# The first sublayer's modulation, norm and projections run by pairs of contraction blocks

## The chip, the cores and the metric

The kernel runs as one program on one core of a Trainium2 chip. The metric is device time in microseconds (us) of one execution; the median of a few runs is compared. TensorE (PE) multiplies matrices, VectorE (DVE) and ScalarE (ACT) work elementwise, GpSimd (POOL) does small elementwise work, and SyncE (SP) issues most of the transfers. Each engine works off its own queue in order and waits on semaphores for the others.

## What is computed

A two-layer transformer block for 256 tokens of width 1024 in float32, followed by a second block (convolutions, neighbourhood attention, a mixture of experts). Only the beginning of the first layer matters here:

```
cond = silu(c)
mod  = cond @ ada_w[0] + ada_b[0]
sh1, sc1, g1, sh2, sc2, g2 = split(mod, 6)
h = x * rsqrt(mean(x*x) + eps) * norm_mix[0] * (1 + sc1) + sh1
u = h @ w_in                       # 1024 x 2976, "even_w_in"
c_q, c_kv, k_r, u_dil = u[:384], u[384:640], u[640:672], u[672:]
q, kv = rms_norm(c_q) @ w_uq, rms_norm(c_kv) @ w_ukv
```

After that come the attention over q, k, v and the dilated attention over u_dil.

## The kernel before

**Weights.** All matrices stream through five buffers of 1 MB (`raw`). `fetch` (L219) issues one transfer on SP for two parts of 512 KB each; `pump(n)` (L253) takes the next parts of one fixed list, `seq`. For a weight part ACT makes a rounded copy (`whi`, L268) and DVE the remainder (`wlo`, L270), and each product is three matmuls (`mm3`, L343: whi with th, wlo with th, whi with tl, where th and tl are the same two halves of the activations). For a part of the modulation matrix (`Ada`) DVE multiplies it with the row silu(c) (`rc`) and sums (`ada_part`, L302): a product of 128x1024 for each block of 128 output columns. When all eight blocks of a vector are there, one small step adds the bias (L312). A buffer is free again when its last DVE step is done.

**Staging.** The list begins with the 16 modulation parts of shift and scale, then come the weights of the projection in six column groups ("ein", 0) to ("ein", 5) of 512 columns (the last has 416), with the smaller matrices `uq` and `ukv` behind the third. Meanwhile PE transposes x, ACT takes the sums of squares (`raw_part`, L459) and DVE the root (`rstd2`, L473); `normT` (L508) then scales the eight transposed blocks with the modulation columns and splits them into th and tl. `proj` (L563) runs one column group over all eight contraction blocks, into two accumulators `pg`, one for each half of the tokens, which `evac` empties on ACT. After group 0 `late_consts` (L866) makes sine and cosine, from which POOL makes the rope tables (`rope_tables`, L657). After group 1 the latents are normed, and after group 2 they are turned and split (`lh`, `ll`) and multiplied with `uq` and `ukv`; groups 3 and 4 follow, and group 5 runs among the attention.

**Setup.** `start` (L782) issues the small transfers on three queues and turns rows of parameters into columns (`turn`: a transpose on PE and a copy on DVE); `rest` turns those that are needed later. Within the rules set by these calls a scheduler fixes each engine's order when the program is built.

Of the kernel before, what the change touches and what calls it, by code (L numbers as in the profile page):

```python
# [37 lines left out]

PACK = {"mlp_w1": (512, "c"), "mlp_w2": (D, "k"), "even_w_in": (512, "k"), "even_w_out": (D, "k"),
        "mla_w_uq": (768, "k"), "mla_w_ukv": (1024, "k"), "odd_w_in": (512, "k"), "odd_w_out": (D, "k"),  # L40
# [4 lines left out]
def packed(w, width, mode):  # L45


    out = []
    for m in w:
        K, N = m.shape  # L50
        m = m.reshape(K // 128, 128, N)
        for c0 in range(0, N, width):
            c = m[:, :, c0:c0 + width]
            if mode == "k":
                per = 2 * max(1, SUB // c.shape[2])
                out += [c[k:k + per].transpose(1, 0, 2).ravel() for k in range(0, len(c), per)]
            else:
                out += [c[:, :, j:j + 256].transpose(1, 0, 2).ravel() for j in range(0, c.shape[2], 256)]
    return np.concatenate(out)
# [50 lines left out]
def dram(ap, off, dims):  # L110
    return bass.AP(tensor=ap.tensor, offset=ap.offset + off, ap=dims)
# [44 lines left out]
class Ada:  # L156
# [3 lines left out]
    def __init__(self, key, src, vec, outs, also=None):  # L160
        self.key, self.src, self.runs = key, src, [(vec, outs)] + ([also] if also else [])
        self.row = key[2] in (2, 5)
        self.n = KB
        self.held = False
        self.raw = {}


class Net:
# [30 lines left out]

    def setup_stream(self, groups):  # L200

        self.seq, self.keys, self.held = [], {}, set()
        for main, side, *late in groups:
            for it in main + side:
                self.keys[it.key] = it
            m, s = ([(it, j) for it in l for j in range(it.n)] for l in (main, side))
            if late:
                late[1] = [it.key for it, _ in m].index(late[1])
                h = len(self.seq) + late[1] + len(s) - late[0]
                self.held |= set(range(h, h + late[0]))  # L210
            self.seq += spread(m, s, *late)
        self.pos = 0
        self.done = 0
# [86 lines left out]
    def ada_part(self, it, j, src):  # L300
        nc = self.nc
        if not it.row:  # L302
            if j == 0:
                it.acc = [self.sm.tile([128, 8], F32, name="msum", tag="msum") for _ in it.runs]
            for r, (vec, (dst, bias, plus)) in enumerate(it.runs):
                acc = it.acc[r]
                out = src if r == len(it.runs) - 1 else self.new_acc()
                self.order(nc.vector.scalar_tensor_tensor(out, src, 1.0, self.crow[vec], op0=ALU.mult, op1=ALU.mult,
                                                          accum_out=acc[:, j:j + 1]))
                if j == it.n - 1:  # L310
                    bias = self.col[bias[0]][:, bias[1]:bias[1] + 8]
                    self.order(nc.vector.scalar_tensor_tensor(dst, acc, plus, bias, op0=ALU.add, op1=ALU.add))  # L312
            return
# [455 lines left out]
    def start(self):  # L769
# [46 lines left out]
        def turn(srcs, t):  # L816
            n = t.shape[0]
            p = self.ps.tile([128, 512], F32, name="pt", tag="t")
            self.tp(p[:, :n], t)
            c = cn.tile([128, n], F32, name=srcs[0][0] + "c")  # L820
            nc.vector.tensor_copy(c, p[:, :n])
            r = 0
            for nm, _, k in srcs:
                self.col[nm] = c[:, r:r + k]
                r += k
            return c

        self.b1s = ExitStack()
        self.b1 = self.b1s.enter_context(self.tc.tile_pool(name="b1", bufs=1, side="right", reuse_waits="tile"))
        self.R0 = self.big.tile([128, D], F32, name="R0", tag="gate", bufs=self.gate_bufs)[:, 0:T]  # L830
        self.crow_tiles(None, ["c"], nc.scalar)
        first = [("c", I["c"], 8)]
        bias = [("ada_b", I["ada_b"], 96)]
        more = [("nmix", I["norm_mix"], 16), ("nmlp", I["norm_mlp"], 16), ("ng", I["norm_g_2"], 32),
                ("c2", I["c_2"], 8), ("cctx", I["c_ctx_2"], 8),
                ("qlat", I["mla_q_lat_norm"], 3), ("kvlat", I["mla_kv_lat_norm"], 2), ("subln", I["diff_subln"], 1)]
        bias2 = [("b_ada_2", I["b_ada_2"], 96)]
        r1 = rows(first, nc.sync)
        nc.scalar.dma_start(self.eye, C["eye"])
        r2 = rows(bias, nc.scalar)  # L840
        for t in range(2):
            nc.gpsimd.dma_start(self.x[:, t], dram(I["x"], t * 128 * D, [[D, 128], [1, D]]))
        r3 = rows(more, nc.gpsimd)
        r4 = rows(bias2, nc.gpsimd)
        cs = cn.tile([128, 24], F32, name="cs")
        self.vec = {"c": cs[:, 0:8], "c2": cs[:, 8:16], "cctx": cs[:, 16:24]}
        nc.scalar.activation(self.vec["c"], turn(first, r1), AF.Silu)
        turn(bias, r2)

        def rest():  # L850
            turn(more, r3)
            turn(bias2, r4)
            nc.scalar.activation(self.vec["c2"], self.col["c2"], AF.Silu)
            nc.scalar.activation(self.vec["cctx"], self.col["cctx"], AF.Silu)

        self.rest = rest
        self.ones = cn.tile([128, 128], F32, name="ones")
# [110 lines left out]
class Block1:  # L968
# [9 lines left out]
    def even_items(self):  # L978
        n = self.n
        a = [self.w_items("even_w_in", ("ein", i), 0, D, 2976, i * 512, min(512, 2976 - i * 512)) for i in range(6)]  # L980
# [4 lines left out]
        return a[:3] + [uq, ukv] + a[3:] + o  # L985

    def even(self):
        n, nc = self.n, self.n.nc
        hT = n.normT(n.x, n.modA(0, 0, n.col["nmix"][:, 0:8]), R=n.R0)
        with ExitStack() as es:  # L990
# [28 lines left out]
            ulat = lat.tile([128, 2, D], F32, name="ulat")  # L1019
            n.proj(("ein", 0), hT, KB, 512, evac(0))  # L1020
            n.late_consts()
            n.proj(("ein", 1), hT, KB, 512, evac(1))
            tmp = n.big.tile([128, 2, D], F32, name="tmp", tag="xn")
# [6 lines left out]
            for t in range(2):  # L1030
                nc.vector.tensor_scalar(tmp[:, t, :384], ulat[:, t, :384], ss[:, 0, t:t + 1], None, op0=ALU.mult)
                nc.vector.tensor_scalar(tmp[:, t, 384:640], ulat[:, t, 384:640], ss[:, 1, t:t + 1], None, op0=ALU.mult)
            n.proj(("ein", 2), hT, KB, 512, evac(2))
            tq, tk, tdq, tdk = (n.rope_tables(g, d, rd, t)
# [76 lines left out]

            dil(3)
            dil(4)
# [1098 lines left out]
def build(ctx, tc, I, C, out, probe=None, upto=99):  # L2212
# [21 lines left out]
    first = net.ada_items(0, 0, [0, 1], "c")  # L2234
    net.setup_stream([([], first)] + [(ws(), *side) for _, ws, *side in steps])
    net.pump(6)
    net.raw_start()
    for t in range(2):
        for hf in range(2):
            net.raw_part(net.x, t, hf)  # L2240
    R = net.spread_rows(net.rstd2(net.raw[1]))
    net.nc.scalar.copy(net.R0, R)
    net.pump(16)
    net.flush()
    net.pump(18)
    net.rest()
    net.hooks = {}
# [73 lines left out]
```

## Time and profile before

| | us |
|---|---|
| runs (three) | 2309.50, 2309.63, 2305.48 |
| median | 2309.5 |
| profiled execution | 2298.07 |
| its span | 2296.2 |
| PE busy in it | 2186.0 (95%) |
| DVE busy in it | 1918.0 (84%) |
| ACT busy in it | 1382.8 (60%) |
| POOL busy in it | 198.9 (9%) |

The span is the profiler's from the first to the last instruction. Busy times are sums over the whole span; a matmul counts as busy while it is in the pipe, so PE may be busy and not at its peak. Waits are told by the engine that ended them.

### The profile page before, as it was taken

How to read it: one execution, taken by the hardware profiler on the slowest of the kernel's cores; microseconds unless marked ns; L12 is line 12 of the kernel's file. 1: busy time of each engine (PE TensorE's matmuls, PEld its weight loads, DVE VectorE, ACT ScalarE, POOL GpSimd, SP SyncE). 2: the span in 40 equal slices, each digit the busy share in tenths (PEclk: the TensorE clock that was granted, in tenths of full speed). 3: DMA queues.
4: the chain of work that ended last, by engine and by line, in shares of the span. 5: the costliest groups of instructions: out<-in, count | busy, mean ns of one | idle time of the engine just before them, and what ended most of it. 6: DMA issues, size and time to landing. Idle time of an engine off the chain costs nothing. (4 is left out here: it accounts for less than half of the span.)

```text
span 2296.2 us, 30679 instructions
## 1 busy us (share of the span) xinstructions
PE 2186.0 (95%) x11405; PEld 1802.1 (78%) x11405; DVE 1918.0 (84%) x2602; ACT 1382.8 (60%) x1890; POOL 198.9 (9%) x280
## 2 busy tenths in 40 slices
PE   4998999999999999999999999999999999999997
PEld 3866888676889886589987888888888788788875
DVE  7887988787997668579856899999898889898996
ACT  4644545546645536254444787787777777777764
POOL 2310010311100121200000000000000000000010
PEclk9988999999999999999999999999999999999998
DMA  8554998643677596279925899999989899898981
GB/s 336 186 173 159 336 356 327 188 165 130 245 283 290 187 335 153 74 290 379 384 99 226 342 353 370 341 368 353 349 327 367 326 367 350 338 360 338 370 309 49
DMA packets 102397, 647.44 MB, mean 282 GB/s; under 512 B 12101, under 2 KB 19749, under 8 KB 28128
## 3 DMA queue, kind: packets, MB, share of 16 engines
q1 hardware_dynamic: 88512, 618.83, 71.3%
q0 software_dynamic: 13040, 25.41, 4.5%
q8 instruction: 91, 1.49, 0.2%
q10 hardware_dynamic: 688, 1.16, 0.2%
q14 instruction: 66, 0.54, 0.1%
HBM read 637.21 MB, written 8.15 MB: 281 GB/s over the span
## 5 line engine op out<-in xcount | busy, mean ns | idle before, releaser
L270 DVE TENSOR_TENSOR wlo<-raw,whi 128x1024 fp32r<-128x1024 f32 (+1 forms) x551 | 662.4, 1228 | 123.2 <-ACT whi L268 115.1
L268 ACT CAST whi<-raw 128x1024 fp32r<-128x1024 f32 (+1 forms) x551 | 562.0, 1049 | 335.7 <-PE pg L347 96.8
L270 DVE TENSOR_TENSOR wlo<-rawm,whi 128x1024 fp32r<-128x1024 f32 x422 | 506.0, 1238 | 37.1 <-ACT whi L268 25.4
L268 ACT CAST whi<-rawm 128x1024 fp32r<-128x1024 f32 x422 | 426.2, 1051 | 82.7 <-PE sc L348 29.9
L346 PE MATMUL pg<-th,whi 128*128 128x256 f32 x1024 | 293.0, 290 | 2.2 <-ACT th L527 1.5
L347 PE MATMUL pg<-tl,whi 128*128 128x256 f32 x1024 | 292.7, 286 | 0.5 <-DVE tl L522 0.5
L348 PE MATMUL pg<-th,wlo 128*128 128x256 f32 x1024 | 292.4, 286 | 0.4 <-DVE wlo L270 0.4
L346 PEld LDWEIGHTS pg<-th,whi 128*128 128x128 f32 x1024 | 197.7, 195 | 8.8 <-issue 3.6
L347 PEld LDWEIGHTS pg<-tl,whi 128*128 128x128 f32 x1024 | 199.5, 195 | 4.4 <-issue 2.0
L348 PEld LDWEIGHTS pg<-th,wlo 128*128 128x128 f32 x1024 | 199.4, 195 | 1.4 <-DVE wlo L270 1.2
L347 PE MATMUL sc<-wlo,xo 128*128 128x512 f32 x448 | 179.1, 400 | 8.4 <-DVE wlo L270 8.4
L347 PE MATMUL sc<-wlo,th 128*128 128x512 f32 x448 | 176.9, 395 | 2.8 <-DVE wlo L270 2.8
L348 PE MATMUL pg<-whi,gg 128*128 128x512 f32 x448 | 176.0, 394 | 3.5 <-PEq L2141 3.5
L347 PE MATMUL pg<-wlo,gg 128*128 128x512 f32 x448 | 178.8, 399 | 0.0
L346 PE MATMUL sc<-whi,xo 128*128 128x512 f32 x448 | 176.9, 395 | 0.0
L346 PE MATMUL sc<-whi,th 128*128 128x512 f32 x448 | 176.3, 394 | 0.0
L348 PE MATMUL sc<-whi,xo 128*128 128x512 f32 x448 | 175.7, 392 | 0.0
L348 PE MATMUL sc<-whi,th 128*128 128x512 f32 x448 | 174.9, 390 | 0.7 <-POOL th L2037 0.7
L346 PE MATMUL pg<-whi,gg 128*128 128x512 f32 x448 | 161.1, 392 | 1.4 <-ACT gg L369 1.4
L347 PE MATMUL po<-wlo,ah 128*128 128x512 f32 x344 | 134.3, 391 | 1.4 <-DVE wlo L270 1.4
L346 PE MATMUL po<-whi,ah 128*128 128x512 f32 x344 | 135.2, 393 | 0.0
L348 PE MATMUL po<-whi,al 128*128 128x512 f32 x344 | 133.9, 389 | 0.0
(587 smaller groups left out, 3888.8 us busy)
## 6 DMA issues: line engine op xcount, KB each, us to landing
rawm<-in_moe_w SPq DMA_DIRECT2D x196, 1024.0 KB, 6.6
raw<-in_moe_w SPq DMA_DIRECT2D x140, 1024.0 KB, 6.3
raw<-in_mlp_w SPq DMA_DIRECT2D x64, 1024.0 KB, 6.7
raw<-in_ada_w SPq DMA_DIRECT2D x48, 1024.0 KB, 7.2
raw<-in_w_ada SPq DMA_DIRECT2D x35, 1024.0 KB, 6.9
raw<-in_ffn_w SPq DMA_DIRECT2D x20, 1024.0 KB, 8.2
rawm<-in_w_ada SPq DMA_DIRECT2D x13, 1024.0 KB, 6.9
rawm<-in_ffn_w SPq DMA_DIRECT2D x13, 1024.0 KB, 8.4
```

The lines of the kernel that those rows point to most:

```text
L268: self.order(self.nc.scalar.copy(h, src))
L270: self.order((self.nc.gpsimd if pool else self.nc.vector).tensor_sub(l, src, h.bitcast(F32)))
L346: mm(out, a[0], b[0], start=start, stop=False, skip_group_check=True)
L347: mm(out, a[0], b[1], start=False, stop=False, skip_group_check=True)
L348: return mm(out, a[1], b[0], start=False, stop=stop, skip_group_check=True)
```

## The change

The first norm and the column groups 0 to 2 run in one loop over four pairs of contraction blocks. For each pair the list now holds two parts of shift, two of scale, two weight parts of 1024 columns (groups 0 and 1 in one) and one of 512 columns (group 2). `Ada` gets `per`, so that the bias step works on two columns at a time. The products of a pair go into six accumulators: two `py` tiles of two banks, and two `pg`. The norm is taken before the loop as a diagonal matrix (`dg`), which PE multiplies with x; ACT scales and shifts (`hf`), rounds (`th`), and DVE takes the remainder (`tl`). Group 3 is projected directly behind the loop's latents, ahead of `uq`. x is fetched on SP ahead of the weights, the condition row c for the columns on POOL, and the broadcast row `rc` behind three small transfers on ACT's queue. `rest` is called after the first pair's matmuls.

```diff
-PACK = {"mlp_w1": (512, "c"), "mlp_w2": (D, "k"), "even_w_in": (512, "k"), "even_w_out": (D, "k"),
+PACK = {"mlp_w1": (512, "c"), "mlp_w2": (D, "k"), "even_w_in": ((D, 512, 512, 512, 416), "k"), "even_w_out": (D, "k"),
...
-                if j == it.n - 1:
-                    bias = self.col[bias[0]][:, bias[1]:bias[1] + 8]
-                    self.order(nc.vector.scalar_tensor_tensor(dst, acc, plus, bias, op0=ALU.add, op1=ALU.add))
+                if (j + 1) % it.per == 0:
+                    a, b = j + 1 - it.per, j + 1
+                    bias = self.col[bias[0]][:, bias[1] + a:bias[1] + b]
+                    self.order(nc.vector.scalar_tensor_tensor(dst[:, a:b], acc[:, a:b], plus, bias, op0=ALU.add, op1=ALU.add))
...
-        self.R0 = self.big.tile([128, D], F32, name="R0", tag="gate", bufs=self.gate_bufs)[:, 0:T]
-        self.crow_tiles(None, ["c"], nc.scalar)
...
-        r1 = rows(first, nc.sync)
         nc.scalar.dma_start(self.eye, C["eye"])
         r2 = rows(bias, nc.scalar)
+        self.crow_tiles(None, ["c"], nc.scalar)
         for t in range(2):
-            nc.gpsimd.dma_start(self.x[:, t], dram(I["x"], t * 128 * D, [[D, 128], [1, D]]))
+            self.order(nc.sync.dma_start(self.x[:, t], dram(I["x"], t * 128 * D, [[D, 128], [1, D]])))
+        r1 = rows(first, nc.gpsimd)
...
-        nc.scalar.activation(self.vec["c"], turn(first, r1), AF.Silu)
-        turn(bias, r2)

         def rest():
+            nc.scalar.activation(self.vec["c"], turn(first, r1), AF.Silu)
             turn(more, r3)
             turn(bias2, r4)
...
+    def first(self, ps, done):
+        n, nc = self.n, self.n.nc
+        hi, lo = (n.big.tile([128, KB, T], F32R, name=nm, tag=nm) for nm in ("th", "tl"))
+        A = n.sm.tile([128, 8], F32, name="mA", tag="mA")
+        B = n.mod[:, 0, 0]
+        dg = n.diag(n.x)
+        (ia, ib) = self.head
+        def turned(p):
+            z = n.ps.tile([128, 2, T], F32, name="pt", tag="t")
+            for k in range(2):
+                for t in range(2):
+                    c = (2 * p + k) * 128
+                    n.mm(z[:, k, t * 128:(t + 1) * 128], n.x[:, t, c:c + 128], dg[:, t])
+            return z
+        z = turned(0)
+        for p in range(KB // 2):
+            s = slice(2 * p, 2 * p + 2)
+            if p == 0:
+                n.pump(1)
+                n.bias()
+            n.pump(7 * p + 4)
+            n.order(nc.vector.tensor_tensor(A[:, s], n.mod[:, 0, 1, s], n.col["nmix"][:, s], ALU.mult))
+            n.pump(7 * p + 5)
+            f = n.big.tile([128, 2, T], F32, name="hf", tag="hf", bufs=2)
+            for i, k in enumerate((2 * p, 2 * p + 1)):
+                n.order(nc.scalar.activation(f[:, i], z[:, i], AF.Identity, scale=A[:, k:k + 1], bias=B[:, k:k + 1]))
+                n.order(nc.scalar.copy(hi[:, k], f[:, i]))
+                n.order(nc.vector.tensor_tensor(lo[:, k], f[:, i], hi[:, k].bitcast(F32), ALU.subtract))
+            n.pump(7 * p + 7)
+            if p < KB // 2 - 1:
+                z = turned(p + 1)
+            for k in (2 * p, 2 * p + 1):
...
+                for g in (2, 0, 1):
+                    for t in range(2):
+                        n.mm3(ps[g][t], (hi[:, k, t * 128:(t + 1) * 128], lo[:, k, t * 128:(t + 1) * 128]), w[g], k == 0, k == KB - 1)
+            if p == 0:
+                n.rest()
...
-            n.proj(("ein", 0), hT, KB, 512, evac(0))
+            hT = self.first([[x[:, 0], x[:, 1]] for x in wide] + [[n.ps.tile([128, 512], F32, name="pg", tag="g") for _ in range(2)]],
+                            [evac(i) for i in range(3)])
             n.late_consts()
-            n.proj(("ein", 1), hT, KB, 512, evac(1))
...
-            n.proj(("ein", 2), hT, KB, 512, evac(2))
+            n.proj(("ein", 3), hT, KB, 512, evac(3))
...
-            dil(3)
             dil(4)
```

DVE's queue at the program's start (`raw,msum<-raw,rc` is a modulation product, `rms` the row norm's small steps). Before, the products lead:

```order
L821 COPY cc<-pt 128x8
L821 COPY ada_bc<-pt 128x96
L308 SCALAR_TENSOR_TENSOR raw,msum<-raw,rc 128x1024 x6
L481 TENSOR_SCALAR rms<-ssq 128x1 x2
L483 TENSOR_SCALAR rms<-rms 128x1 x2
```

In the changed program, from the last of the norm's steps on:

```order
L442 SCALAR_TENSOR_TENSOR rms<-rms 128x1 x2
L453 TENSOR_SCALAR dg<-eye,rms 128x128 x2
L312 SCALAR_TENSOR_TENSOR raw,msum<-raw,rc 128x1024
L826 COPY ada_bc<-pt 128x112
L312 SCALAR_TENSOR_TENSOR raw,msum<-raw,rc 128x1024
```

The whole norm moved ahead of the first product.

DVE's queue behind the first pair in the changed program (`cc`, `nmlpc` and `b_ada_2c` are what `rest` copies; PE's transposes for them stand behind the first pair's 36 matmuls):

```order
L274 TENSOR_TENSOR wlo<-raw,whi 128x1024
L1022 TENSOR_TENSOR tl<-hf,th 128x256 x2
L274 TENSOR_TENSOR wlo<-raw,whi 128x1024 x2
L826 COPY cc<-pt 128x8
L826 COPY nmlpc<-pt 128x70
L826 COPY b_ada_2c<-pt 128x96
L312 SCALAR_TENSOR_TENSOR raw,msum<-raw,rc 128x1024 x2
L317 SCALAR_TENSOR_TENSOR mod<-msum,ada_bc 128x2
```

Before, the same copies lay between products, and PE's transposes for them ahead of every weight matmul. Now they lie between PE's first burst and the second pair's products.

ACT's queue around sine and cosine, before (`ulat` and `ud` are what `evac` fills):

```order
L361 COPY ulat<-pg 128x512
L268 CAST whi<-raw 128x1024
L1026 ACTIVATE tmp,lss<-ulat 128x384
L268 CAST whi<-raw 128x1024
L404 ACTIVATE sin<-ang 128x64
L409 ACTIVATE cos<-angt 128x64
```

And in the changed program:

```order
L272 CAST whi<-raw 128x1024 x5
L1056 COPY ud<-pg 128x512 x2
L366 COPY ulat<-py 128x512 x2
L1078 ACTIVATE tmp,lss<-ulat 128x384
L366 COPY ulat<-py 128x160
L1056 COPY ud<-py 128x352
L1079 ACTIVATE tmp,lss<-ulat 128x256
L1078 ACTIVATE tmp,lss<-ulat 128x384
L1056 COPY ud<-py 128x352
L409 ACTIVATE sin<-ang 128x64
L414 ACTIVATE cos<-angt 128x64
```

The cosine moved from behind group 0 to behind the emptying of all three groups.

## Rows read from the trace of the kernel before

**Rows 1.** Stages: us, busy time of each engine, granted clock, DMA share, GB/s.

```profile
13.20:38.00 24.80, 5.52 (x23) 3.79 (x21) 24.49 (x63) 6.72 (x15) 6.21 (x11) 1.00 1.01 396
38.00:62.00 24.00, 23.82 (x96) 18.88 (x97) 22.11 (x50) 16.24 (x27) 5.04 (x15) 1.00 0.68 260
62.00:73.30 11.30, 11.30 (x51) 9.12 (x50) 5.85 (x20) 4.41 (x11) 7.92 (x33) 1.00 0.27 94
73.30:113.00 39.70, 38.98 (x199) 32.49 (x198) 36.67 (x58) 29.46 (x40) 5.84 (x5) 1.00 0.61 216
113.00:140.00 27.00, 25.00 (x173) 21.82 (x171) 26.89 (x50) 14.26 (x39) 7.33 (x9) 1.00 0.44 152
140.00:200.00 60.00, 54.19 (x228) 33.74 (x229) 43.17 (x84) 22.63 (x50) 0.00 (x0) 0.77 0.52 180
```

**Rows 2.** DVE in order of time: start, duration, line, out<-in, idle before.

```profile
13.22 1.22 DVE L308 SCALAR_TENSOR_TENSOR raw<-raw,rc 128x1024 f32<-128x1024 f32 x1
...
20.10 0.33 DVE L481 TENSOR_SCALAR rms<-ssq 128x1 f32<-128x1 f32 x2
...
22.28 1.22 DVE L308 SCALAR_TENSOR_TENSOR raw<-raw,rc 128x1024 f32<-128x1024 f32 x1
```

**Rows 3.** Transfers: issuing queue, count, size, us from issue to landing.

```profile
rc<-in_c ACTq DMA_DIRECT2D x1, 512.0 KB, 4.5
...
eye<-const_eye ACTq DMA_DIRECT2D x1, 64.0 KB, 8.3
stage<-in_ada_b ACTq DMA_DIRECT2D x1, 48.0 KB, 10.9
```

**Rows 4.** ACT at the start: the Silu of the row, the first square.

```profile
5.29 1.06 ACT L896 ACTIVATE rc<-rc 128x1024 f32<-128x1024 f32 x1 [1.88 <-DMA rc<-in_c]
...
11.30 0.63 ACT L467 ACTIVATE raw<-x 128x512 f32<-128x512 f32 x1 [0.99 <-DMA x<-in_x]
```

**Rows 5.** PE's first weight matmuls in order of time.

```profile
38.99 0.63 PE L348 MATMUL pg<-whi,tl 128*128 128x512 f32 x1
...
39.42 0.63 PE L346 MATMUL pg<-whi,th 128*128 128x512 f32 x1
...
43.44 0.39 PE L348 MATMUL pg<-whi,tl 128*128 128x512 f32 x1
...
43.66 0.39 PE L346 MATMUL pg<-whi,th 128*128 128x512 f32 x1
```

**Rows 6.** A transpose of the setup on PE and its copy on DVE.

```profile
9.62 0.24 PE L355 MATMUL pt<-eye,stage 8*128 8x8 f32 x1 [9.62 <-DMA eye<-const_eye]
9.90 0.17 DVE L821 COPY cc<-pt 128x8 f32<-128x8 f32 x1 [0.16 <-PE pt L355]
```

**Rows 7.** Weight rows, casts and the splitting of activations on DVE and ACT.

```profile
43.24 4.83 ACT L268 CAST whi<-raw 128x1024 fp32r<-128x1024 f32 x5
...
44.31 5.77 DVE L270 TENSOR_TENSOR wlo<-raw,whi 128x1024 fp32r<-128x1024 f32 x5 [0.45 <-ACT whi L268]
...
74.92 0.43 DVE L560 TENSOR_TENSOR ll<-hf,lh 128x256 fp32r<-128x256 f32 x1
...
75.46 0.48 ACT L556 ACTIVATE hf<-pt,nmixc 128x256 f32<-128x256 f32 x1 [0.54 <-DVE ll L560]
```

**Rows 8.** The cosine on ACT, and DVE's two kr steps that wait for POOL's tables.

```profile
56.63 0.26 ACT L409 ACTIVATE cos<-angt 128x64 f32<-128x64 f32 x1 [1.25 <-DVE angt L408]
...
63.21 0.23 DVE L1052 TENSOR_TENSOR kr<-ulat,tkA 128x64 f32<-128x64 f32 x1 [0.55 <-POOL tkA L669]
...
69.21 0.23 DVE L1053 TENSOR_TENSOR kr<-kr,kt 128x64 f32<-128x64 f32 x1 [4.23 <-POOL kt L681]
```

**Rows 9.** DVE's marks behind the latents: first lh, qss, second hss.

```profile
74.59 0.29 DVE L559 CAST lh<-hf 128x256 fp32r<-128x256 f32 x1 [0.98 <-ACT hf L556]
...
85.54 1.74 DVE L1088 TENSOR_REDUCE qss<-tmp 128x16 f32<-128x1536 f32 x1
...
112.80 1.75 DVE L693 TENSOR_REDUCE hss<-tmp 128x24 f32<-128x1536 f32 x1
```

More of the change, by code (lines that the diff above doesn't have):

```diff
@@ L48, in packed @@
     out = []
+    widths = width if isinstance(width, tuple) else (w.shape[2] // width) * (width,)
+    assert sum(widths) == w.shape[2]
     for m in w:
@@ L51, in packed @@
         m = m.reshape(K // 128, 128, N)
-        for c0 in range(0, N, width):
+        for i, width in enumerate(widths):
+            c0 = sum(widths[:i])
             c = m[:, :, c0:c0 + width]
@@ L162, in __init__ @@
         self.row = key[2] in (2, 5)
-        self.n = KB
+        self.n = self.per = KB
         self.held = False
@@ L196, in probe, with setup_stream @@
             self.nc.gpsimd.dma_start(self.probe_out[name], ap)
-    def setup_stream(self, groups):
-        self.seq, self.keys, self.held = [], {}, set()
+    def setup_stream(self, head, groups):
+        self.seq, self.keys, self.held = list(head), {it.key: it for it, _ in head}, set()
         for main, side, *late in groups:
@@ L820, in turn @@
             c = cn.tile([128, n], F32, name=srcs[0][0] + "c")
-            nc.vector.tensor_copy(c, p[:, :n])
+            self.order(nc.vector.tensor_copy(c, p[:, :n]))
             r = 0
@@ L829, in start @@
         self.b1 = self.b1s.enter_context(self.tc.tile_pool(name="b1", bufs=1, side="right", reuse_waits="tile"))
-        self.R0 = self.big.tile([128, D], F32, name="R0", tag="gate", bufs=self.gate_bufs)[:, 0:T]
-        self.crow_tiles(None, ["c"], nc.scalar)
         first = [("c", I["c"], 8)]
-        bias = [("ada_b", I["ada_b"], 96)]
-        more = [("nmix", I["norm_mix"], 16), ("nmlp", I["norm_mlp"], 16), ("ng", I["norm_g_2"], 32),
+        bias = [("ada_b", I["ada_b"], 96), ("nmix", I["norm_mix"], 16)]
+        more = [("nmlp", I["norm_mlp"], 16), ("ng", I["norm_g_2"], 32),
                 ("c2", I["c_2"], 8), ("cctx", I["c_ctx_2"], 8),
@@ L854, in rest @@
             nc.scalar.activation(self.vec["cctx"], self.col["cctx"], AF.Silu)
-        self.rest = rest
+        self.rest, self.bias = rest, lambda: turn(bias, r2)
         self.ones = cn.tile([128, 128], F32, name="ones")
@@ L979, in even_items @@
         n = self.n
-        a = [self.w_items("even_w_in", ("ein", i), 0, D, 2976, i * 512, min(512, 2976 - i * 512)) for i in range(6)]
+        a = [self.w_items("even_w_in", ("ein", i), 0, D, 2976, i * 512, w) for i, w in ((0, D), (2, 512), (3, 512), (4, 512), (5, 416))]
+        self.head = a[:2]
         uq = Chunk(("uq",), (n.I["mla_w_uq"], 0), 3, 768, "k")
@@ L984, in even_items @@
              for i, k in ((0, 4), (1, 2))]
-        return a[:3] + [uq, ukv] + a[3:] + o
+        return a[2:3] + [uq, ukv] + a[3:] + o
+    def first(self, ps, done):
[30 more added lines that the diff above has]
+            for k in (2 * p, 2 * p + 1):
+                (ah, al), (bh, bl) = ia.parts[k], ib.parts[p]
+                w = [(ah[:, 0, :512], al[:, 0, :512]), (ah[:, 0, 512:], al[:, 0, 512:]), (bh[:, k % 2], bl[:, k % 2])]
+                for g in (2, 0, 1):
[3 more added lines that the diff above has]
+                n.rest()
+        for g in (2, 0, 1):
+            for t in range(2):
+                done[g](t, ps[g][t])
+        return hi, lo
     def even(self):
         n, nc = self.n, self.n.nc
-        hT = n.normT(n.x, n.modA(0, 0, n.col["nmix"][:, 0:8]), R=n.R0)
         with ExitStack() as es:
@@ L1019, in even @@
             ulat = lat.tile([128, 2, D], F32, name="ulat")
-            n.proj(("ein", 0), hT, KB, 512, evac(0))
+            wide = [n.pa.tile([128, 2, 512], F32, name="py", tag="acc") for _ in range(2)]
+            hT = self.first([[x[:, 0], x[:, 1]] for x in wide] + [[n.ps.tile([128, 512], F32, name="pg", tag="g") for _ in range(2)]],
+                            [evac(i) for i in range(3)])
             n.late_consts()
-            n.proj(("ein", 1), hT, KB, 512, evac(1))
             tmp = n.big.tile([128, 2, D], F32, name="tmp", tag="xn")
@@ L2234, in build @@
     first = net.ada_items(0, 0, [0, 1], "c")
[L2235 to L2246, printed above, removed]
+    for it in first:
+        it.per = 2
+    groups = [(ws(), *side) for _, ws, *side in steps]
+    wide, narrow = b1.head
+    head = []
+    for p in range(KB // 2):
+        head += [(it, 2 * p + j) for it in (*first, wide) for j in range(2)] + [(narrow, p)]
+    net.setup_stream(head, groups)
     net.hooks = {}
```

## The prediction

> **What bounds the kernel now.** I read the stages first [rows 1], then the queues inside the first 113 us. The program differs from the one before only up to about 200 us; from PE's last attention transposes on, every engine's instructions stand in the same order. So the change is worth what it moves in that head, and the remaining 2096 us are carried along unchanged. In the head VectorE (DVE) is the engine that is late. From 13.2 to 38 us it is busy 24.49 of 24.80, with the modulation columns and the row norm; DMA is full as well (share 1.01), but every landed megabyte waits for DVE. TensorE (PE) is busy 5.52 of these 24.80 and starts its first projection at 38. From 113 to 140 DVE is busy 26.89 of 27.00. In between, from 38 to 113, DVE has 10.4 us free (1.9, 5.5 and 3.0 in the three rows). A change that lets PE start early therefore gains only what it takes off DVE's work, or out of DVE's waits, up to 113.
>
> **The start.** DVE's first modulation product starts at 13.22 now [rows 2]. The change puts the row norm ahead of it, in DVE's order and in ScalarE's (ACT): the Silu of the condition row, four squares, 16 small DVE steps and two diagonals. The condition row now leaves ACT's DMA queue as fourth, behind the unit matrix, the biases and the norm weights, where it was first. As first it landed 4.5 us after its issue, and the third of that queue after 10.9 [rows 3]. Issued at about 2.1 it lands between 6.6 and 13.0. I take 10.2, because the unit matrix and the biases needed 3 to 4 us each behind it, while the activations lead SP's queue and are there sooner. The Silu takes 1.06, the four squares 0.63 each [rows 4], the 16 steps 0.1 each (22 took 2.2, from 20.10 to 22.28 [rows 2]), the diagonals about 0.3: 10.2 + 1.1 + 2.5 + 1.6 + 0.3 gives **15.7**, and 12.1 to 18.5 by the bounds.
>
> The Trainium skill, "DMA: Bandwidth & Descriptors", section on queues, rings and completion order, says that an engine takes descriptors of one ring in order and changes between rings at packets. By that rule the row cannot overtake the three that now stand ahead of it, and the nearer end is the late one; the rows agree, since the unit matrix landed behind the row although it is an eighth of its size [rows 3].
>
> **The four pairs.** One pair costs DVE four products of 1.15 (six took 6.9 us [rows 2]), four small steps of 0.4 together, three weight rows of 1.15 (five took 5.77) and two of the low parts of 0.35 (the 0.43 of the row, overlapped) [rows 7]: 9.15. Behind the columns ACT must make hf, th, hf, th (four of 0.43) and then the cast of the next weights (0.97) before the second weight row may start, 2.75 after the columns, when DVE has filled only 2.0 of it. So a pair takes 9.9; pair 0, which also copies the biases, takes 10.2 and ends at 25.9.
>
> Then comes a wait which the profile of before doesn't have. The closing setup (three transposes and three copies of small rows) moved from between the products to behind pair 0's 36 matmuls on PE, and DVE's three copies stand ahead of pair 1's products. PE starts pair 0 at 21.9, when its columns and th are there. The first matmuls of a burst stood 0.43 apart (512 columns at 1.2 GHz) and later ones 0.23 (2.4 GHz) [rows 5]. Pair 0 waits at 26.0 for its narrow weight row with 25 matmuls left: 26.0 + 25 x 0.23 = 31.7. Three rounds of transpose and copy at 0.6 each (0.45 in the rows, and the way back [rows 6]) give 33.5. **DVE stands still for 7.6 us.** Queued behind it are pair 1's products, and behind these SP's fetches, which wait for the buffers. Bounds: 36 matmuls at 0.23 end at 30.2, at 0.43 at 37.4; I take the mixed value, since the row shows this change of pace in the same kind of burst. From 33.5 three pairs of 9.9 end at **63.2**. DMA has landed what they need by then: at the 396 GB/s of the first stage [rows 1] a megabyte takes 2.7 us, so a buffer released at 35.8 is filled again well ahead of its use at 45.8.
>
> The Trainium skill, "TensorE: Matmul & The Clock Gate", section on HAM oscillation, says that matmuls in bursts with waits between them begin each burst at half rate. It speaks against this change. The row agrees for a burst's beginning: 0.43 at 39, 0.23 at 43, [rows 5], in a stage whose granted clock reads 1.00 [rows 1]. By it pairs 2 and 3 would each lose another 1.6 us of PE time, which ends in the next wait below and adds nothing to the sum; what it makes of pair 0 is a rival.
>
> **From the pairs to the latents.** PE has 17 matmuls behind the last weight row: 63.2 + 17 x 0.23 = 67.1. All three projections end together, so ACT empties six accumulators in a row, and only behind them comes the cosine: seven steps of about 0.45 put its end at 70.2, where it is 56.89 now [rows 8]. POOL builds its tables from it: 6.3 us to the one that the first kr step needs (56.89 to 63.2), 12.3 to kr's second step (69.21) [rows 8]. In the changed order DVE's first kr step stands ahead of the latents' scaling and of four weight rows. It is reached at 71.5 and waits until 76.5, **5.0 us**. From there 7.6 us of DVE work follow (four weight rows, 3.8; the latents' scaling and small steps, 3.8), to 84.1, past kr's second wait at 82.5. The fourth quarter of the next projection (512 columns, now ahead of the latents) needs a weight row at 79.7; its 12 matmuls end at 82.4 (0.23) to 84.8 (0.43), and I take 84.0, since PE has waited 4 us. The first lh cast comes 1.6 later, at **85.7**; it is at 74.59 now [rows 9].
>
> **What comes back.** That projection is already done: 48 matmuls (10.9 us) on PE and four weight rows (4.6) on DVE which before lay behind lh. From lh to the qss reduction it is 10.95 now (74.59 to 85.54 [rows 9]), set by the up projection on PE, and unchanged: 96.6. From there to 112.80 DVE runs 27.3 without a gap; four rows less make 22.7: **119.3 against 112.8, +6.5**. PE stands at +0.5: 85.7 + 0.5 to the up projection, and then as before less one projection, the last fourth starting at 99.3 for 98.6 now. The row scaling that falls away on DVE (eight steps of 0.4) is simply absent from the 9.15. From 113 to 140 DVE is full, so the +6.5 stays; behind 200 us nothing differs.
>
> The profiled execution took 2298.1 us, the median of the three runs is 2309.5. The sum in the profiled execution is 2298.1 + 6.5 = 2304.6; carried to the median it is **2316.0**. By its own bounds (start -3.6 to +2.8, pair 0 -1.5 to +5.7, the fourth quarter -1.6 to +0.8, the ACT wait of a pair 0 instead of 0.75, -2.3 in three) it lies at 2311 to 2321.
>
> **Rivals.** (1) PE, not DVE, ends the attention stage. From 140 to 200 PE is busy 54.19 of 60 and DVE 43.17, and DVE's 17 free microseconds could take up its lateness; then only PE's +0.5 is left: **2310**, no change. Against it: PE waits there for softmax rows which DVE makes. It decides if DVE's free time in 140 to 200 shrinks by 6. (2) Faster: TensorE's level. Its granted clock in 140 to 200 is 0.77 [rows 1]; at full speed 54.19 x 0.23 = 12.5 us of it would go. If the other arrangement of transposes and scores keeps it up, 6.5 - 12.5 gives **2303.5**. For it: the transposes and scores of two units now stand closer. Against it: the same matmuls with the same partners. It decides from a granted clock over 0.9 in this stage. (3) Pair 0 never comes to the fast pace, because it waits for weight rows while it starts: 36 x 0.43 ends it at 37.4, +5.7, **2321.7**.
>
> **Chances.** Forecast 0.47, rival 1 0.28, rival 2 0.10, rival 3 0.15. A measurement of this kernel can tell about 0.2%, 4.6 us, from no change. Of the forecast 0.07 lies within that, of rival 1 0.02 below and 0.26 within: faster 0.12, same 0.33, slower 0.55. The range takes in rivals 1 and 3 and reaches to rival 2: 2303 to 2324.
>
> **What would show it.** First weight matmul near 22 us; DVE idle 7 to 8 us ahead of the copy into cc; the first projection's end at 67 and the cosine at 70; DVE idle about 5 us for POOL ahead of kr; first lh near 86, the first score reduction near 121. If DVE doesn't wait at the copy, or starts its products near 12, the step is wrong and the result is no change or a gain; if all these come and the last attention stage still starts no later than now, it is rival 1.

## The result

The changed kernel takes 2326.8 us in the median of six runs (2320.6 to 2335.2), the kernel before 2305.8 in six (2302.1 to 2309.6): 1.0101 times as long, 95% interval 1.0077 to 1.0126. It is slower, as forecast, but by 21 us and not by 6.5, and outside the range, which ended at 2324. The profiled execution took 2330.3 us (span 2328.4), 32 us more than that of before. That one was a quick run of its kernel: 80 runs of before, taken beside the experiments below, have a median of 2306.1.

The stages of [rows 1] in the changed kernel (us, busy time of PE, PEld, DVE, ACT, POOL, granted clock, DMA share, GB/s), and as the last line a stage that is used throughout: from DVE's k norm (`k<-k,qss`) to the first weight matmul of the next sublayer, the attention with its output projection.

```profile
13.20:38.00 24.80, 16.14 (x62) 12.52 (x63) 13.80 (x43) 8.45 (x17) 1.70 (x3) 1.00 0.70 254
38.00:62.00 24.00, 18.88 (x77) 15.07 (x76) 21.75 (x40) 9.59 (x14) 0.00 (x0) 0.79 0.86 326
73.30:113.00 39.70, 34.47 (x155) 28.81 (x155) 30.96 (x66) 25.18 (x45) 20.31 (x52) 0.96 0.51 188
140.00:200.00 60.00, 54.83 (x235) 36.13 (x233) 37.77 (x79) 17.28 (x44) 0.00 (x0) 0.61 0.52 184
119.88:247.72 127.84, 110.28 (x490) 76.59 (x491) 88.75 (x184) 49.18 (x111) 10.35 (x12) 0.75 0.42 149
```

The same stage in the kernel before:

```profile
106.15:222.47 116.32, 105.00 (x529) 74.96 (x528) 89.43 (x185) 53.74 (x116) 10.36 (x12) 0.87 0.49 173
```

PE starts 13 us earlier, but DVE, busy 24.49 of the first 24.80 us in [rows 1], is busy only 13.80 now. The k norm comes at 119.88 where it came at 106.15: **13.7 us of lateness from the head**. The stage behind it holds 39 matmuls fewer and takes 127.8 us where it took 116.3: **11.5 us more**, at a granted clock of 0.75 for 0.87. With two levels, 1.2 and 2.4 GHz, that is 2 x 0.25 x 127.8 = 64 us at the lower one, for 30. The clock of the whole execution, which every run gives, points the same way: 0.965 to 0.970 in the six runs of the changed kernel, 0.971 to 0.980 in the 80 of before. Behind this stage the two profiles differ by 7 us more, which I don't count to the change: from there to the end it took 2074 us in before, 2081 here, and 2070 to 2084 in its variants below, so one profile differs from another there by as much.

DVE's marks in the changed kernel, in order of time (start, duration, line, out<-in, idle before and what ended it). They answer [rows 2], [rows 8] and [rows 9]:

```profile
17.58 1.22 DVE L312 SCALAR_TENSOR_TENSOR raw<-raw,rc 128x1024 f32<-128x1024 f32 x1
...
35.83 0.17 DVE L826 COPY cc<-pt 128x8 f32<-128x8 f32 x1 [6.38 <-PE pt L360]
...
37.17 1.22 DVE L312 SCALAR_TENSOR_TENSOR raw<-raw,rc 128x1024 f32<-128x1024 f32 x1
...
45.42 2.36 DVE L274 TENSOR_TENSOR wlo<-raw,whi 128x1024 fp32r<-128x1024 f32 x2 [0.52 <-ACT whi L272]
...
47.69 1.22 DVE L312 SCALAR_TENSOR_TENSOR raw<-raw,rc 128x1024 f32<-128x1024 f32 x1
...
79.75 0.27 DVE L1104 TENSOR_TENSOR kr<-ulat,tkA 128x64 f32<-128x64 f32 x1 [2.94 <-POOL tkA L674]
...
88.65 0.23 DVE L1105 TENSOR_TENSOR kr<-kr,kt 128x64 f32<-128x64 f32 x1 [2.20 <-POOL kt L686]
...
90.00 0.28 DVE L564 CAST lh<-hf 128x256 fp32r<-128x256 f32 x1
...
102.41 1.74 DVE L1140 TENSOR_REDUCE qss<-tmp 128x16 f32<-128x1536 f32 x1
...
119.88 1.76 DVE L1145 TENSOR_TENSOR k<-k,qss 128x1536 f32<-128x1536 f32 x1
```

The wait ahead of `cc` and the first of the two ahead of `kr` stand where the prediction put them; the second is one that it had not. ACT's queue at the start, as transfers (count, size, us from issue to landing) and as the Silu of the row; they answer [rows 3, 4]:

```profile
rc<-in_c ACTq DMA_DIRECT2D x1, 512.0 KB, 9.3
...
eye<-const_eye ACTq DMA_DIRECT2D x1, 64.0 KB, 4.7
stage<-in_ada_b ACTq DMA_DIRECT2D x1, 48.0 KB, 5.6
```

```profile
11.43 1.06 ACT L899 ACTIVATE rc<-rc 128x1024 f32<-128x1024 f32 x1 [7.53 <-DMA rc<-in_c]
```

### The profile page after: what moved, and what is told of

It is laid out like the page before. It is cut to its first block, busy times and chain, and to the rows that moved or that the text cites. A ratio compares the mean times of both kernels' runs of the same rounds, so it can differ in the third digit from the quotient of the medians.

```text
span 2328.4 us, 30702 instructions
## 1 busy us (share of the span) xinstructions
PE 2208.3 (95%) x11417; PEld 1818.1 (78%) x11417; DVE 1918.2 (82%) x2605; ACT 1382.3 (59%) x1893; POOL 197.8 (8%) x278
## 5 line engine op out<-in xcount | busy, mean ns | idle before, releaser
L274 DVE TENSOR_TENSOR wlo<-raw,whi 128x1024 fp32r<-128x1024 f32 (+2 forms) x551 | 662.5, 1228 | 124.4 <-ACT whi L272 116.6
L272 ACT CAST whi<-raw 128x1024 fp32r<-128x1024 f32 (+2 forms) x551 | 561.2, 1049 | 327.1 <-PE pg L352 83.7
```

The source lines that it names most:

```text
L272: self.order(self.nc.scalar.copy(h, src))
L274: self.order((self.nc.gpsimd if pool else self.nc.vector).tensor_sub(l, src, h.bitcast(F32)))
```

## Experiments

All kernels in one table. "Above before" and the ratio are to the runs of before on the same chip (medians of 2304.3 to 2307.3); "stage" is the one from the k norm to the next sublayer, with its granted clock. The marks and the stage are from one profile each. The intervals are some 5 us wide to either side of the middle, so whole times that differ by a few us are not told apart.

| kernel | median us | above before | ratio, 95% interval | first product | first lh | k norm | stage | clock |
|---|---|---|---|---|---|---|---|---|
| before | 2306.1 | 0 | 1 | 13.2 | 74.6 | 106.2 | 116.3 | 0.87 |
| changed | 2326.8 | 21.0 | 1.0101 (1.0077 to 1.0126) | 17.6 | 90.0 | 119.9 | 127.8 | 0.75 |
| e1 rest early | 2320.8 | 14.2 | 1.0067 (1.0046 to 1.0088) | 17.3 | 85.7 | 116.2 | 128.8 | 0.75 |
| e6 rc first | 2321.9 | 14.6 | 1.0071 (1.0050 to 1.0092) | 12.4 | 85.7 | 115.6 | 128.6 | 0.76 |
| e7 cosine at the start | 2319.1 | 11.8 | 1.0064 (1.0040 to 1.0088) | 17.0 | 84.9 | 113.3 | 126.8 | 0.78 |
| e2 cosine behind pair 1 | 2334.4 | 27.8 | 1.0114 (1.0076 to 1.0153) | 17.7 | 97.2 | 125.6 | 126.9 | 0.78 |
| e4 e1, e2 and e6 | 2317.7 | 11.1 | 1.0052 (1.0029 to 1.0075) | 12.4 | 84.8 | 113.2 | 128.9 | 0.73 |
| g1 e1, e6 and e7 | 2309.7 | 5.4 | 1.0021 (0.9999 to 1.0043) | 12.8 | 75.6 | 104.0 | 128.2 | 0.76 |
| e3 group 3 back | 2321.1 | 14.5 | 1.0078 (1.0053 to 1.0103) | 17.5 | 86.6 | 124.3 | 122.3 | 0.80 |
| g2 g1 and e3 | 2305.6 | 1.3 | 1.0002 (0.9980 to 1.0023) | 12.4 | 71.5 | 109.9 | 119.4 | 0.83 |
| f1 48 matmuls more | 2322.3 | 18.0 | 1.0071 (1.0039 to 1.0102) | 17.3 | 90.1 | 120.0 | 119.0 | 0.88 |
| d1 before, delayed, a tile of 4 bytes more | 2341.7 | 37.4 | 1.0154 (1.0121 to 1.0187) | 13.3 | 89.1 | 120.7 | 123.4 | 0.80 |
| d2 before, delayed, a tile of 64 bytes more | 2338.8 | 32.4 | 1.0140 (1.0126 to 1.0155) | 13.2 | 89.7 | 121.3 | 118.3 | 0.85 |
| d3 before, delayed | 2320.4 | 13.1 | 1.0057 (1.0032 to 1.0081) | 13.2 | 88.2 | 119.8 | 115.7 | 0.86 |
| h3 before, 48 matmuls more | 2305.3 | -1.1 | 0.9988 (0.9972 to 1.0004) | 13.3 | 75.0 | 106.6 | 120.8 | 0.89 |
| h1 g2, casts ahead | 2304.2 | -2.2 | 0.9990 (0.9970 to 1.0010) | 12.6 | 68.8 | 106.9 | 120.2 | 0.82 |
| h2 h1, 24 matmuls more | 2297.4 | -9.0 | 0.9955 (0.9943 to 0.9968) | 12.6 | 68.3 | 106.2 | 112.8 | 0.92 |

### The steps of the head, one at a time

**The setup ahead of the first weight matmuls (e1).**

```diff
                 n.bias()
+                n.rest()
...
-            if p == 0:
-                n.rest()
```

> The changed kernel with the closing setup (three transposes and copies) called right behind the copy of the biases, ahead of the first weight matmuls. In the changed kernel DVE stood 6.4 us ahead of the copy into cc and restarted at 37.2. Theory H (the head): that wait is on the path. It falls to about 1 us, pair 1 starts near 30.5, the first lh cast comes near 83.5 instead of 90.0, and the time falls by 6 to 7 us to about 2320 (2326.8 before it); if the granted clock of the attention stage (0.61 from 140 to 200 us) recovers with it, to about 2309. Theory C (the clock): half of the loss of 21 us is the clock of the attention stage and comes from the order of work there, not from the head; then the stage keeps about 0.6 and the time is 2320. Rival D: the weight rows of pair 1 have not landed and DVE waits for DMA instead; pair 1 still starts at 36 to 37 and nothing changes.

Pair 1 starts at 31.1 instead of 37.2, as expected, but lh comes only 4.3 us earlier: the first wait for POOL, fed by the late cosine, grows from 2.94 to 4.54.

```profile
20.15 0.17 DVE L826 COPY cc<-pt 128x8 f32<-128x8 f32 x1 [0.36 <-PE pt L360]
...
31.06 1.22 DVE L312 SCALAR_TENSOR_TENSOR raw<-raw,rc 128x1024 f32<-128x1024 f32 x1
...
75.10 0.25 DVE L1103 TENSOR_TENSOR kr<-ulat,tkA 128x64 f32<-128x64 f32 x1 [4.54 <-POOL tkA L674]
```

The kernel stands 14.2 us above before instead of 21.0. The wait at `cc` was on the path, and rival D falls. The clock of the attention does not recover.

**The row first on its queue (e6).** `crow_tiles` goes ahead of the load of `eye`, as it stood before the change.

> The changed kernel with the row rc first on ACT's queue, and nothing else. It prices the step of the start by itself: the first product comes at 12.5 instead of 17.6. If the head is DVE's all the way, everything up to the k norm moves by the same 5 us (k norm near 115) and the time falls by 4 to 5 us to about 2322. Rival: DVE's wait ahead of the copy into cc grows by what the start gives, because PE's first pair waits for weights from DMA; then the k norm gains 1 to 2 us and the time is about 2326.

First product 12.4 (5.2 earlier), k norm 115.6 (4.3 earlier), 14.6 us above before instead of 21.0. The head moves with its start, but for 0.9 us.

**The cosine at the start (e7).** Positions and frequencies are loaded on ACT's queue, and `sin_of` is worked out behind pair 0.

> The changed kernel with positions and frequencies loaded at the start and sine and cosine worked out behind the first pair, the masks where they were. It prices the step of the late cosine by itself: DVE's waits for POOL ahead of kr (2.9 and 2.2 us) go, the fourth column group still ends on PE near 85, and the first lh comes at 87 to 88.5 instead of 90.0. The time falls by 2 to 3 us to about 2324.

The cosine comes at 31.6, the waits for POOL ahead of `kr` shrink to 0.4, and the k norm comes 6.6 us earlier (11.8 us above before), more than I expected: lh comes 5.1 us earlier, since group 3's last weight row stands behind the first `kr` and that wait held PE as well, and the up projection behind it takes 10.9 us to `qss` instead of 12.4. In the changed kernel PE stood 3.13 us for lh and began at the lower level (granted clock 0.53 from 90.33 to 93.70, its matmuls of 384 columns 0.32 us apart and later 0.17); in e7 that wait is gone, and the clock is 1.00 from the first of them on. PE in the changed kernel:

```profile
90.33 0.53 PE L351 MATMUL py<-whi,lh 128*128 128x384 f32 x1 [3.13 <-DVE lh L564]
...
93.12 0.52 PE L351 MATMUL py<-whi,lh 128*128 128x384 f32 x1
93.44 0.52 PE L352 MATMUL py<-wlo,lh 128*128 128x384 f32 x1
...
94.56 0.33 PE L351 MATMUL py<-whi,lh 128*128 128x384 f32 x1
94.73 0.33 PE L352 MATMUL py<-wlo,lh 128*128 128x384 f32 x1
```

**The cosine behind pair 1 (e2), and with the other two edits (e4).**

```diff
             n.pump(7 * p + 7)
+            if p == 1:
+                n.late_consts()
```

> The changed kernel with the constants of sine and cosine made behind the second pair instead of behind the emptying of the six accumulators. In the changed kernel DVE waited 2.9 and 2.2 us for POOL's tables ahead of kr. Theory H: both waits fall away; the first lh cast comes 2 to 4 us earlier (86 to 88 instead of 90.0), no more, since the fourth column group ends on PE at 85; the time falls by 2 to 4 us to about 2324. Rival: DVE's small steps between the products cost as much as the waits, and nothing changes (2327).

> The changed kernel with three edits: the setup ahead of the first weight matmuls, the constants of sine and cosine behind the second pair, and the row rc first on ACT's queue again. Theory H: the start moves from 17.6 to about 12.5 us, the wait at cc (6.4) and those for POOL go; lh comes near 76, as late as in the kernel before (74.6), the lateness at 140 us falls from 13 to about 0, and the time to about 2306 to 2310 if the clock of the attention stage comes back to 0.77 with it. Theory C (the clock's fall comes from the order of work in the attention stage): the stage keeps a granted clock near 0.6 and the time stays near 2315 to 2317.

Both have a new wait. In e2:

```profile
58.39 0.56 DVE L877 CAST masks<-xn 128x768 bf16<-128x768 f32 x1 [10.02 <-DMA xn<-const_masks]
```

The masks land in `xn`, and there the diagonal matrix lies until PE's last transposes; in DVE's order their cast stood ahead of pair 2. e2 got slower by it, and e4 kept 9.2 us of the same wait. So these two don't tell about POOL's tables; e7 does, where the masks stay behind the loop.

**All three steps (g1).**

> The changed kernel with the head repaired: the row rc first on ACT's queue, the setup ahead of the first weight matmuls, and the constants of sine and cosine loaded at the start on ACT's queue and worked out behind the first pair (the masks stay where they are, since their landing place is held by the diagonal matrix until the last pair; that hold cost the two kernels with the early cosine a wait of 9 to 10 us on DVE). First product 12.4, four pairs end near 58, first lh near 76 and the k norm at 103 to 107, as in the kernel before (106.15). Theory H (only the head's lateness costs): about the time of the kernel before, 2304 to 2309. Theory O (the attention stage has lost 11 us by the order of its own work): the stage takes 127 us again, with about 65 us at the low level, and the time is 2315 to 2319.

The k norm comes at 104.0, 15.9 us earlier; the three alone gave 3.7, 4.3 and 6.6, 14.6 in sum. The time is 2309.7, 5.4 us above before. But the stage behind it takes 128.2 us at 0.76, as in the changed kernel: a head on time does not bring the clock back.

### Lateness or order

**The same lateness in the kernel before (d1, d2, d3).** Eleven reductions of 128x1024 on DVE stand ahead of the weight rows, their result unused. In d1 and d2 it went to a new tile of 4 and of 64 bytes, in d3 into a column that is there already.

```diff
+    junk = net.raw[1][:, 0, 0:1]
+    for _ in range(11):
+        net.order(net.nc.vector.reduce_max(junk, net.x[:, 0], axis=AX.X))
```

> The kernel before, with eleven reductions of 128x1024 on DVE (about 1.15 us each, 12.6 together, results unused) behind the modulation columns and ahead of the first weight rows: a head that is late, and nothing else changed. Theory L (lateness alone lowers the clock of the attention stage): the stage from the k norm to the first matmul of the next sublayer takes 126 to 128 us instead of 116.3, its time at the low level is near 65 us instead of 31, and the time is about 2306.6 + 10 + 11 = 2328. Theory O (the order of the work in the stage decides, not when it starts): the stage keeps its 116 us and about 31 us of low level, and the time is 2306.6 plus the delay that remains at the k norm (8 to 12.6): 2315 to 2319.

> The kernel before with the eleven extra reductions on DVE again, their result now in a tile of 64 bytes for each partition. With the tile of 4 bytes TensorE's matmuls of 512 columns stood 0.233 us apart over the whole program instead of 0.227, so that run was not a clean delay. If the 4 bytes were the cause (all later tiles moved by them), the spacing is 0.227 again. Theory L (lateness alone lowers the level in the attention stage): the stage from the k norm to the next sublayer takes 126 to 128 us with about 65 us at the low level, and the time is 2304 + 14 + 11 = about 2329. Theory O (the order of work in the changed kernel's attention does it): 116 to 118 us with about 31, and the time is 2304 + 14 = about 2318.

> The kernel before with the eleven extra reductions on DVE, their result in a column that exists already, so that no tile of the program moves. In the two runs with a tile of their own the matmuls of 512 columns stood 0.233 us apart in the whole program, where all other kernels have 0.227. If the added tile is the cause, the spacing is 0.227 here. Then this is the clean delay: Theory O (the order of the work in the changed attention lowers the level) gives a stage of 116 to 119 us with 30 to 36 us at the low level and 2305 + 14 = 2319; Theory L (lateness) gives 126 to 128, about 65, and 2329.

d3 is the clean one. Its k norm is as late as that of the changed kernel (119.80 and 119.88), and its stage is that of before:

```profile
119.80:235.48 115.68, 104.84 (x530) 74.92 (x528) 89.67 (x186) 53.71 (x116) 10.36 (x12) 0.86 0.50 174
```

It takes 2320.4, 13.1 us above before (7 to 19 by the interval), for 13.65 us at the k norm. The clock of its whole execution is 0.972 to 0.978 in all eight runs, as in before. Theory L falls: by the medians the lateness is carried to the end one for one, and the level in the attention is not its doing. What the changed kernel loses beyond that, 8 us by the medians (21.0 less 13.1), 10 by the ratios, 11.5 in the profiles, belongs to the changed order. d1 and d2 are slowed over the whole program by something else, told in the last section; d1's stage took 123.4 us, so the order of before doesn't always give 116.

**Group 3 back behind uq and ukv (e3, and g2 on the repaired head).**

```diff
-        return a[2:3] + [uq, ukv] + a[3:] + o
+        return [uq, ukv] + a[2:] + o
...
-            n.proj(("ein", 3), hT, KB, 512, evac(3))
...
+            dil(3)
             dil(4)
```

> The changed kernel with column group 3 put back behind uq and ukv, as it was before the change. Theory H: work is only moved; lh comes near 84 instead of 90.0, the four weight rows and 48 matmuls come back behind it, and at 140 us the lateness is within 2 us of the changed kernel's 13; the time is 2325 to 2328 if the clock of the attention stage stays near 0.6. Theory C in the form that the earlier group 3 takes away the matmuls that filled PE's gaps from 120 to 140 us: the granted clock from 140 to 200 goes back to 0.75 or more, and 8 to 11 us come back: about 2317.

> The same repaired head, with column group 3 back behind uq and ukv. In the changed kernel that edit alone shortened the stage from the k norm to the next sublayer from 127.8 to 122.3 us, with 48.6 us of low level instead of 65, and made the k norm 4.4 us later. Theory H: as with the repaired head alone, 2304 to 2310. Theory O: the stage at 122, the k norm near 108: 2312 to 2315, some 3 us under the repaired head alone.

The stage holds 530 matmuls again and takes 122.3 and 119.4 us instead of 127.8 and 128.2, at a clock of 0.80 and 0.83: 5.5 and 8.7 us back of the stage's 11.5. In the traces of both, the stage's work stands in the order of before again: ACT's 116 instructions exactly, DVE's 187 but for one or two, PE's matmuls but for a few records, no more than before and its delayed kernels differ among themselves. So the place of group 3 is all that the change did to the stage's order. The order of before took 115.7 to 123.4 us in seven profiles (before, d1, d2, d3, e3, g2, h1), the changed one 126.8 to 128.9 in seven (changed, e1, e2, e4, e6, e7, g1). The k norm comes 4.4 and 5.8 later when group 3's work lies behind lh, so of the stage's gain 1.1 and 2.9 us are left in the profiles; the whole time falls by 6.5 and 4.1 by the medians, and no more can be read from it. g2 stands level with the kernel before.

**More matmuls in the attention (f1, and h3 on the kernel before).**

```diff
                     n.tick(4)
+                    z = n.ps.tile([128, 512], F32, name="fill", tag="t")
+                    for _ in range(8):
+                        n.mm(z, n.eyeb, n.masks[:, :512])
```

> The changed kernel with eight more matmuls of 512 columns (the identity with the masks, results unused) in each of six steps of the attention: 48 more, 10.6 us at 0.22 each. If the low level in the changed kernel's attention (65 us between 100 us and the next sublayer) is what costs the stage its 11 us, and more work on TensorE keeps it at the high level, the low time falls below 30 us, and the stage gets shorter although it does more: 120 us or less instead of 127.8, total about 2319. If the level is not reached that way, the stage gets 8 to 12 us longer: about 2336.

> The kernel before with the 48 extra matmuls in its attention. If the low level of that stage (31 us in the profile of before) costs there what it costs in the changed kernel, the low time falls under 15 us, and the stage is 116 + 10.9 - 0.5 x 20 = about the same; the time is then 2302 to 2306. If the level of this stage does not matter, the 10.9 us are simply added: 2312 to 2315.

f1's stage:

```profile
120.04:239.06 119.02, 106.61 (x534) 73.08 (x539) 89.18 (x185) 49.16 (x111) 10.36 (x12) 0.88 0.45 160
```

With 48 useless matmuls more it is 8.8 us shorter than the changed kernel's, at 0.88 for 0.75, and the clock of the whole execution is 0.972 to 0.976 in its five runs. Same lateness, more work, less time: that speaks for the level as the cause of the stage's loss. It doesn't isolate it, since the scheduler also put some six of DVE's steps and some 70 of PE's other matmuls elsewhere. By the medians it gains 3 us only (18.0 above before instead of 21.0), by the ratios 7, and the intervals overlap. In the kernel before, which loses less to the level, the same 48 make the stage 4.5 us longer in the profile and the whole time no different (2305.3).

### A version that beats both

> The repaired head with column group 3 behind uq and ukv (2305.6 before it), and in each pair the second wide weight part cast and subtracted ahead of the activations, so that DVE has work while ACT makes hf and th. In the repaired kernel DVE waits 0.5 us for th and 0.5 for the next cast in each pair. If DVE sets the head, four pairs end 4 us earlier, the first lh comes near 67.5 instead of 71.5, and the time falls by 3 to 4 us to about 2302. Rival: the kr steps wait for POOL or the latents for PE, and nothing changes.

> The same with four extra matmuls of 512 columns in each of six steps of the attention (24, 5.4 us at 0.227). With eight in the changed kernel the low level fell from 65 to 28.5 us and the stage from 127.8 to 119.0 us. If four do as much, the low time of about 41 falls to about 20, the stage from 119 to about 114, and the time to about 2298, which is under the kernel before; if they do not hold the level, it is 2 to 5 us above the same kernel without them.

h1 has `n.pump(7 * p + 6)` for `n.pump(7 * p + 5)`: lh comes 2.7 us earlier, the time does not move measurably. h2, with four extra matmuls in each step, takes 2297.4: 0.9955 of before, 0.9943 to 0.9968, 9 us faster. Its k norm is on time and its stage shorter than that of before (here too the scheduler moved a few other instructions, so not all of it need be the fillers'):

```profile
106.19:218.98 112.79, 103.83 (x549) 73.66 (x553) 89.65 (x186) 53.84 (x116) 10.31 (x12) 0.92 0.51 178
```

## Why the prediction was wrong, point by point

- **The mechanism of the head** was right, step by step: the late row, DVE's stand at `cc`, the cosine behind the evacuations, POOL ahead of `kr`. Its sizes were too small. The forecast had lh at 85.7 and 6.5 us left at the end of the head; it was 90.0, and 13.7 at the k norm. (At the `hss` of the forecast it was 9.0, 121.79 for 112.80, but steps that lay ahead of that mark now lie behind it; at the next sublayer's first product it was 14.5, 158.85 for 144.36.)
- **The start**: 15.7 forecast, 17.58 measured, inside its bounds. The row landed at 11.4 for 10.2, as the last of the transfers shown, and the row norm behind it took 6.1 for 5.5. In e6 the step is worth 4.3 us at the k norm.
- **The pairs**: 9.9 forecast, 10.5 measured (37.17 to 47.69). The wait for ACT is 0.48 for th and 0.52 for the cast, 1.0 and not 0.75; pair 0 took 11.9 for 10.2, mostly since the copy of the biases waits 1.0 for its transpose.
- **The stand at `cc`**: 7.6 forecast; DVE has nothing to do for 7.2 of the 7.7 us from 29.4 to 37.17. PE's first burst took 10.4 for 9.8. This term was right, and rival 3 did not happen: the spacing went to 0.23 at 29 us.
- **The cosine and POOL**: forecast one wait of 5.0, measured 2.9 and 2.2. The sum was right, but the second one stood where the prediction had none, directly ahead of lh.
- **From lh on**: the up projection took 12.4 us to `qss` for 10.95, since PE had waited for lh and began at the lower level. Up to the k norm 3.1 us came back for 4.6 in the sum, as one of the four weight rows had stood behind it before. With lh's 4.3 these are the 7.2 us between 6.5 and 13.7.
- **The step that failed** is the last one: "From 113 to 140 DVE is full, so the +6.5 stays; behind 200 us nothing differs." It left TensorE's level out of the sum. I had its row, 0.77 from 140 to 200 [rows 1], and priced it in rival 2, but only upward, to 1.00. "The same matmuls with the same partners" was my argument against a change of the level. It does not follow: with the order of before the stage runs at 0.80 to 0.87, early or late (d3), with that of the changed kernel at 0.73 to 0.78, late or early (g1). By d3 the head's lateness alone gives 2320.4, inside the range; the stage's 11.5 us took the time out of it.
- **Where the stage loses**: group 3, moved ahead, took 39 matmuls out of the stage, and moved steps of the dilated attention ahead of the first score reduction. That was forecast near 121 and came at 133.71, 13.8 us behind the k norm where it was 8.3. But up to DVE's first product for the next sublayer this cost 0.8 us only. The other 10.8 are lost behind it, with as many matmuls and the same DVE work, at a clock of 0.69 for 0.82. The stage in these two parts, changed and then before:

```profile
119.88:158.85 38.97, 33.36 (x201) 27.30 (x202) 34.30 (x70) 15.99 (x42) 7.33 (x9) 0.87 0.37 137
158.85:247.72 88.87, 76.92 (x291) 49.28 (x290) 54.45 (x117) 33.19 (x69) 3.02 (x3) 0.69 0.44 154
```

```profile
106.15:144.36 38.21, 36.22 (x240) 30.70 (x239) 34.88 (x71) 21.38 (x49) 7.33 (x9) 0.96 0.48 167
144.36:222.47 78.11, 68.79 (x291) 44.26 (x290) 54.55 (x117) 32.36 (x67) 3.03 (x3) 0.82 0.50 175
```

- **Waits and the level**: the Trainium skill, "TensorE: Matmul & The Clock Gate", section on HAM oscillation, says that waits for data between bursts of matmuls bring the half rate back; I cited it for the pairs only. In the attention the traces agree with it in part. PE idles 17.6 us in the changed stage (127.84 less 110.28) at 0.75 and 11.3 before at 0.87, but 11.2 and 10.8 in e3 and g2 at 0.80 and 0.83, and 12.4 in f1 at 0.88: the sum of the idle time does not give the level.
- **The bounds** that the prediction lists add up to -9.0 and +9.3, which is 2307 to 2325 if all fall on one side; its 2311 to 2321 has no working. Its PE marks, 99.3 for 98.6, make 0.7 and not 0.5.
- **Rival 1** (DVE's free time takes the lateness up) falls with d3: by the medians all of it stays. From 140 to 200 DVE's free time grew from 16.8 to 22.2 us, where this rival wanted it 6 us smaller.

What is open: why the place of group 3 leaves the level lower for the rest of the stage. With group 3 back the stage still takes 119.4 to 122.3 us, for 116.3 in before, though its order is the same. d1 and d2, which keep that order too and differ by a tile's size, took 123.4 and 118.3 (both with matmuls further apart, told below), so these 3 to 6 us need be no sign of anything else in the change. What makes one order differ so much from profile to profile is open as well.

## What to carry to other kernels

Lateness in the head was carried to the end one for one here, so read each step of a restructured head against the engine that is late, with the waits behind it: one repaired wait made the next one longer. Matmuls that are moved ahead of a stage in which TensorE waits are also taken out of that stage, and a scheduler may order the rest of it anew; look at the granted clock there first, and price it in both directions. Where a stage runs at the lower level between waits, even useless matmuls in its gaps can pay (2297.4 for 2304.2 in h2 and h1), and can pay nothing (h3).

## What the runs showed of the hardware

**The level of the attention stage differs widely.** The granted clock there lies between 0.73 and 0.92, with 16 us of difference in the stage between kernels whose DVE work is the same (88.8 to 89.7 us). With one and the same order of work it lies between 0.80 and 0.87, with up to 7.7 us of difference.

**A new tile slowed TensorE's whole program.** In d1 and d2 the matmuls of 512 columns stand 0.233 us apart from the first projection on to the end, in d3 and all other kernels 0.227 to 0.228. Those of 256 columns stand closer in d1 and d2, 0.117 to 0.118 for 0.120. PE in d2, then in d3, in the same late stage:

```profile
1500.00 0.39 PE L348 MATMUL sc<-whi,xo 128*128 128x512 f32 x1
1500.23 0.39 PE L346 MATMUL sc<-whi,xo 128*128 128x512 f32 x1
1500.46 0.40 PE L347 MATMUL sc<-wlo,xo 128*128 128x512 f32 x1
1500.70 0.39 PE L348 MATMUL sc<-whi,xo 128*128 128x512 f32 x1
```

```profile
1499.99 0.39 PE L347 MATMUL sc<-wlo,xo 128*128 128x512 f32 x1
1500.21 0.39 PE L348 MATMUL sc<-whi,xo 128*128 128x512 f32 x1
1500.44 0.39 PE L346 MATMUL sc<-whi,xo 128*128 128x512 f32 x1
1500.67 0.39 PE L347 MATMUL sc<-wlo,xo 128*128 128x512 f32 x1
```

These three kernels have the same instructions and differ in that one tile; d1 and d2 take some 20 us more than d3 (21 and 18 by the medians). A tile of 64 bytes does it like one of 4. Which tile's new place matters was not tried. An added scratch tile is therefore not a neutral probe: look at the matmul spacing before reading such a run.
